# First channel tile of a layer's modulation: dot products moved from VectorE to TensorE

## The chip, the cores and the metric

The kernel runs on one core of a Trainium2 chip. Five engines work side by side: TensorE (PE in the profile, its weight loads PEld), VectorE (DVE), ScalarE (ACT), GpSimd (POOL) and SyncE (SP), which issues most of the transfers between the main memory and the on-chip memory. The metric is the device time of one execution in microseconds (us), lower is better; the median of three runs stands for a kernel.

## The reference

One layer of a latent generator over 512 tokens (8 rows by 64 columns) and 256 context tokens, 1024 channels, fp32 throughout. What matters here is how it opens:

```python
m = silu(c) @ w_mod + b_mod                 # (3072,) -> shift, scale, gate; the same with c_ctx
h  = rmsnorm(x,   pre_g) * (1 + sc)   + sh      # x: 512 x 1024
hc = rmsnorm(ctx, pre_g) * (1 + sc_c) + sh_c    # ctx: 256 x 1024
parts = split(h @ w_in)                     # 1024 x 10240: conv branch, q, k, v, gates
# gated short convolution; neighbourhood attention with rotary, bias and the context's keys;
# two output projections, sigmoid merge, @ w_o, rmsnorm, x + gate * ...
```

Scale and shift are one number per channel. In the kernel channels lie on the 128 partitions, eight channel tiles k = 0 to 7, so tile k needs 128 scales and 128 shifts, each a sum over 1024 products of silu(c) and a column of `w_mod`.

## The kernel before, in words

Weights and activations are split into two parts of a rounded fp32 format (H the rounded value, L the rest), and a projection is three products: H times h, L times h, H times the rest of h. The first stage makes h and, while it does, the first six of the projection's 128-channel units; these accumulate in six PSUM banks `acc[0]` to `acc[5]` over the eight channel tiles.

**The opening.** It runs in a block whose order on PE, DVE, ACT and SP is the order in which it is written. SP loads four tiles of x (128 tokens by 1024 channels, 512 KB each), then `sp` (small vectors: gains, biases), then for k = 0, 1, 2 two slabs of the transposed `w_mod` (128 channels by 1024, 512 KB each, tiles `wm`; slab 8 + k for the scale, k for the shift) and the first weights `fraw` (384 KB). ACT loads the row `crow` of c and applies SiLU. `spread` (line 507) multiplies it by a column of ones, so that it stands on all 128 partitions, and `kept` (L511) copies that to `cb`. Each x tile is normed: the sum of squares (`square`: DVE for tiles 0 and 1, ACT for 2 and 3), `root` on ACT, `norm` (reciprocal and a multiplication: DVE, but ACT, L503, for tile 3). PE turns channel tiles 0 and 1 of each x tile (L539), four x tiles into one PSUM bank per channel tile. Between these stand products whose result nobody reads (`keep_busy`, L516, the identity times 256 columns of `cb`).

**One channel tile.** `condition(k, 0, [0])` and `[1]` (L412) are a DVE instruction each: slab times `cb`, summed along the row, with the bias as starting value; L546 multiplies the scale by the gain. `cast_first` (ACT, L441) makes H of the first weights, `rest_first` (DVE, L445) makes L. ACT applies scale and shift to the turned tile twice (L555), once rounded to h and once exact to `m`; DVE takes the difference (L556). Then `steps(k)` on PE: six products of H and h (L457), six of L and h (L460), six of H and the rest (L463). Behind it PE turns channel tile k + 2 (L450). DVE works one tile ahead: in round k it does the tile's L, the scale of tile k + 1, the rest of h, and at the start of the next round that tile's shift.

**Later.** The context's modulation uses the same DVE instruction with c_ctx (`modulate_c`), for the eight tiles in the order 5, 6, 7, 4, 0, 1, 2, 3, and loads slabs for k below 5 once more. Outside the ordered block a planner that works with costs and due times places the instructions.

The lines that matter in the opening:

```python
for k in range(3): load_slab(k); load_first(k)
...
condition(0, 0, [0])
for t in range(4): keep_busy(1 if t < 2 else 2); # turn x tile t, channel tiles 0 and 1
keep_busy(3)
for k in range(KT):
    cast_first(k); condition(k, 0, [1])
```

## Time and profile before

| what | us |
|---|---|
| median of three runs | 703.24 (702.34 to 703.30) |
| the profiled execution, its own time | 702.93 |
| span of the profile (first to last instruction) | 701.1 |
| between the two, outside the span | 1.8 |

In the rows that follow, a row of the chain of waits gives a start, a length and who was busy; a row of the timeline gives start, length, engine, line, operation, the tiles written and read, and how many instructions; square brackets hold the idle time ahead of it and what ended it. A tile's name stands before its arrow where it is written. A product of two fp32 operands appears as two PE records, and so as two passes; a turned tile as one. The end of a PE record lies after the point at which the next one starts, since products are pipelined.

### The profile page before, as it was taken

Reading aid. Unit: us, or ns where it says so; the run is one execution under the profiler, and the core shown is the slowest. Engines: PE = TensorE matmul, PEld = TensorE weight load, DVE = VectorE, ACT = ScalarE, POOL = GpSimd, SP = SyncE. Lnnn points to the kernel's source line nnn. Section 1 sums busy time; section 2 is a strip of 40 time slices with the busy share of each in tenths; the row PEclk is TensorE's granted clock in tenths of the full one; section 3 lists DMA queues with packets and bytes.
Section 4 is the critical chain, followed back from the end, with each engine's and each line's share of the span. In section 5 each row is a group of like instructions: output and inputs, shape, how many; then the busy total and the mean of one; then the engine's idle time right before and its main releaser. Section 6 shows DMA issues by size and latency. Waiting matters only on the chain.

```text
span 701.1 us, 12064 instructions
## 1 busy us (share of the span) xinstructions
PE 691.2 (99%) x4340; PEld 622.7 (89%) x4340; DVE 609.6 (87%) x1184; ACT 448.2 (64%) x905; POOL 66.6 (9%) x110
## 2 busy tenths in 40 slices
PE   7999999999999999999999999999999999999996
PEld 5888888899989999898999989999898899988885
DVE  6999998799898899977999697999799787775996
ACT  7568542677688677675877757788593444442563
POOL 0000003121040310403103113000000000000000
PEclk9999999999999999999999999999999999999999
DMA  9995854347264463553635436334464445660013
GB/s 352 406 352 189 310 177 125 76 115 189 76 151 110 112 178 121 112 149 81 164 120 136 110 105 160 95 113 135 148 229 136 143 148 176 225 241 30 31 61 120
DMA packets 51727, 108.84 MB, mean 155 GB/s; under 512 B 6610, under 2 KB 6866, under 8 KB 51668
## 3 DMA queue, kind: packets, MB, share of 16 engines
q1 hardware_dynamic: 43202, 92.73, 38.6%
q0 software_dynamic: 8320, 15.21, 10.9%
q8 instruction: 34, 0.56, 0.4%
q14 instruction: 25, 0.20, 0.1%
q10 hardware_dynamic: 146, 0.14, 0.1%
HBM read 87.60 MB, written 5.25 MB: 132 GB/s over the span
## 4 chain that ended last, share of the span: by engine, by line
PE 89%; DVE 6%; ACT 2%; DMA 1%; issue 1%; SPq 0%; ACTq 0%; DVEq 0%
PE ps L299 29%; PE ps L174 8%; PE ps L175 8%; PE ps L176 8%; PE ps L187 6%; PE ps L1042 5%; PE ps L779 3%; PE ps L760 3%; PE ps L192 3%; PE ps L723 3%; PE ps L206 2%; PE ps L457 2%; DVE w L71 2%; PE ps L460 2%; PE ps L463 2%; PE ps L211 1%
## 5 line engine op out<-in xcount | busy, mean ns | idle before, releaser
L71 DVE TENSOR_TENSOR w<-ring,w 128x512 fp32r<-128x512 f32 (+1 forms) x215 | 165.8, 788 | 29.2 <-ACT w L68 27.6
L68 ACT CAST w<-ring 128x512 fp32r<-128x512 f32 (+1 forms) x215 | 144.7, 706 | 67.6 <-PE ps L176 22.3
L299 PE MATMUL ps<-S,w 128*128 128x256 f32 x1152 | 146.2, 283 | 0.2 <-ACT g L315 0.2
L299 PEld LDWEIGHTS ps<-S,w 128*128 128x128 f32 x1152 | 141.7, 192 | 0.4 <-ACT g L315 0.4
L299 PE MATMUL ps<-h,w 128*128 128x256 f32 x864 | 112.6, 284 | 0.2 <-DVE tc L316 0.2
L299 PEld LDWEIGHTS ps<-h,w 128*128 128x128 f32 x864 | 108.0, 191 | 2.4 <-DVE tc L316 0.5
L174 PE MATMUL ps<-h,w 128*128 128x512 f32 x144 | 56.4, 391 | 0.0
L175 PE MATMUL ps<-h,w 128*128 128x512 f32 x144 | 56.2, 390 | 0.0
L176 PE MATMUL ps<-h,w 128*128 128x512 f32 x144 | 55.9, 389 | 0.0
L631 POOL DMA_DIRECT2D tc<-tb x32 | 28.6, 1047 | 285.9 <-DVE tc L629 186.1
L753 ACT ACTIVATE pt<-pt,z 128x512 f32<-128x512 f32 x64 | 43.0, 724 | 7.3 <-DVE z L751 7.1
L68 ACT CAST TH<-ps 128x512 fp32r<-128x512 f32 x64 | 35.8, 586 | 12.1 <-PE ps L760 12.1
L71 DVE TENSOR_TENSOR TL<-ps,TH 128x512 fp32r<-128x512 f32 x64 | 42.5, 681 | 1.0 <-ACT TH L68 0.6
L739 DVE CUSTOM_DVE_ANT_1 ps<-ps,bt 128x512 f32<-128x512 f32 x56 | 38.7, 693 | 4.5 <-PE ps L723 4.3
L760 PE MATMUL ps<-ident,pt 128*128 128x128 f32 x256 | 33.3, 273 | 0.0
L187 PE MATMUL ps<-w,h 128*128 128x512 f32 x128 | 32.4, 394 | 0.0
L176 PEld LDWEIGHTS ps<-h,w 128*128 128x128 f32 x144 | 27.0, 188 | 5.7
L174 PEld LDWEIGHTS ps<-h,w 128*128 128x128 f32 x144 | 27.0, 188 | 5.5
L175 PEld LDWEIGHTS ps<-h,w 128*128 128x128 f32 x144 | 27.0, 188 | 5.5
L746 ACT ACTIVATE pt<-ps,m 128x512 f32<-128x512 f32 x32 | 22.1, 690 | 14.3 <-DVE m L739 13.6
L760 PEld LDWEIGHTS ps<-ident,pt 128*128 128x128 f32 x256 | 29.2, 140 | 2.2 <-ACT pt L753 0.4
L187 PEld LDWEIGHTS ps<-w,h 128*128 128x128 f32 x128 | 23.2, 188 | 4.4
(251 smaller groups left out, 1378.4 us busy)
## 6 DMA issues: line engine op xcount, KB each, us to landing
ring<-in_win SPq DMA_DIRECT2D x148, 256.0 KB, 3.2
wm<-in_wmod SPq DMA_DIRECT2D x26, 512.0 KB, 7.8
ring<-in_wout SPq DMA_DIRECT2D x32, 256.0 KB, 3.1
bt<-in_rel SPq DMA_DIRECT2D x16, 256.0 KB, 2.7
tc<-tb POOLq DMA_DIRECT2D x32, 128.0 KB, 3.6
wg<-in_wmod SPq DMA_DIRECT2D x16, 256.0 KB, 3.3
B<-in_wo SPq DMA_DIRECT2D x8, 512.0 KB, 5.9
fraw<-in_wfirst SPq DMA_DIRECT2D x8, 384.0 KB, 8.5
```

What stands on the lines that cost most here:

```text
L68: cast = nc.scalar.copy(H, src)
L71: nc.vector.tensor_sub(L, src, H.bitcast(F32))
L174: nc.tensor.matmul(ps, lhsT=H[k][:, cs], rhs=mH[k], start=k == 0, stop=False)
L175: nc.tensor.matmul(ps, lhsT=H[k][:, cs], rhs=mL[k], start=False, stop=False)
L176: nc.tensor.matmul(ps, lhsT=L[k][:, cs], rhs=mH[k], start=False, stop=k == KT - 1)
L187: nc.tensor.matmul(ps, lhsT=mH[k][:, ts], rhs=both[k].rearrange("p a c -> p (a c)"), start=k == 0, stop=False, skip_group_check=True,)
L299: nc.tensor.matmul(ps, lhsT=w[:, x, k], rhs=act[y][k], start=start and k + o == 0, stop=k == 3 and o == 2, skip_group_check=True,)
L631: nc.gpsimd.dma_start(x[i::2], u[1 - i::2], accum_op=ALU.add, max_dma_last_dim=2048)
L739: nc.vector.tensor_tensor_reduce(out=s3, in0=s3, in1=bt[:, e::4 - e][:, 0:2], scale=-1.0, scalar=3.0e38, op0=ALU.add, op1=ALU.min, accum_o ...
L753: nc.scalar.mul(x, x, z[:, i:i + 1])
L760: nc.tensor.transpose(tp[:, c], pt[:, c * P:(c + 1) * P], ident)
L1042: nc.tensor.matmul(out, lhsT=a(x, k, ts), rhs=w[y][k // 2][:, k % 2, cols], start=start and k + o == 0, stop=k == 3 and o == 2, skip_group ...
```

## The change

For channel tile 0 the scale and shift of x and of the context come from TensorE. `w_mod` for these 128 scales and 128 shifts lies untransposed in a new input `wmod0` (input channels on partitions, eight blocks of 128); `columns` holds c and c_ctx as columns (128 by 8 by 2). SiLU is applied to `columns` on ACT, behind that of `crow`. `condition0` multiplies, for each of the eight blocks and for scale and shift, a 128 by 128 block of `wmod0` (as weights) by two columns: 16 fp32 products, summed in `acc[1]` (scales) and `acc[2]` (shifts), column 0 for x, column 1 for the context. `finish0` reads the sums: bias and gain by one DVE instruction for the scale, the bias by another for the shift.

What goes with it: the slabs of k = 0 are loaded as four transfers of 256 KB instead of two of 512 KB; ACT issues a second transfer (8 KB) before its SiLU; norm of x tile 3 is on DVE; the H of the first weights of k = 0 is made on DVE; `spread` writes to `acc[3]` and `acc[4]`; `kept` stands later on ACT; nine `keep_busy` products become six; the context's tile 0 takes `colc`, so its two DVE reductions and the second load of its two slabs are gone.

```diff
+        columns = st.tile([P, KT, 2], F32, name="columns")
+        slab0 = []
+        def load_slab0():
+            for i in range(2):
+                t = st.tile([P, D], F32, name="wm", bufs=6).rearrange("p (b v c) -> p b v c", b=4, v=2)
+                slab0.append(t)
+                for n in range(2):
+                    nc.sync.dma_start(t[:, 2 * n:2 * n + 2], wmod0[:, 4 * i + 2 * n:4 * i + 2 * n + 2])
+        def condition0(blocks):
+            for b in blocks:
+                for v in range(2):
+                    nc.tensor.matmul(
+                        acc[1 + v][:, :2], lhsT=slab0[b // 4][:, b % 4, v], rhs=columns[:, b], start=b == 0, stop=b == KT - 1
+                    )
...
-            nc.scalar.copy(H, raws[k])
+            if k == 0:
+                nc.vector.tensor_copy(H, raws[k])
+            else:
+                nc.scalar.copy(H, raws[k])
...
             nc.scalar.dma_start(crow, cc[0:1].rearrange("o (a n) -> o a n", a=2))
+            nc.scalar.dma_start(columns, ccol)
...
-            for k in range(3):
+            load_slab0()
+            load_first(0)
+            for k in range(1, 3):
...
             nc.scalar.activation(crow, crow, AF.Silu)
+            nc.scalar.activation(columns, columns, AF.Silu)
...
-                if i < 3:
-                    nc.vector.tensor_scalar(out=xn[i], in0=xn[i], scalar1=top, scalar2=None, op0=ALU.mult)
-                else:
-                    nc.scalar.mul(xn[i], xn[i], top)
+                nc.vector.tensor_scalar(out=xn[i], in0=xn[i], scalar1=top, scalar2=None, op0=ALU.mult)
...
-                ps = tps()
+                ps = acc[3 + i]
...
-            condition(0, 0, [0])
...
-            for t in range(4):
-                keep_busy(1 if t < 2 else 2)
-            keep_busy(3)
+            keep_busy(1)
+            turn_tile(0)
+            keep_busy(1)
+            turn_tile(1)
+            condition0((0, 1))
+            keep_busy(1)
+            condition0((2, 3))
+            turn_tile(2)
+            condition0((4, 5))
+            keep_busy(1)
+            condition0((6, 7))
+            turn_tile(3)
+            keep_busy(2)
...
+            def finish0(v):
+                nc.vector.tensor_scalar(
+                    out=cols[0, v][:, 0:1], in0=acc[1][:, v:v + 1], scalar1=bsc1[:, 0:1], scalar2=sp[:, PG:PG + 1],
+                    op0=ALU.add, op1=ALU.mult,
+                )
+                nc.vector.tensor_add(cols[0, v][:, 1:2], acc[2][:, v:v + 1], sp[:, BM:BM + 1])
+            finish0(0)
             for k in range(KT):
                 cast_first(k)
-                condition(k, 0, [1])
+                if k:
+                    condition(k, 0, [1])
+                    nc.vector.tensor_mul(cols[k, 0][:, 0:1], cols[k, 0][:, 0:1], sp[:, PG + k:PG + k + 1])
+                else:
+                    finish0(1)
...
         def modulate_c(k):
-            if k < 5:
-                load_slab(k)
-            condition(k, 1)
-            nc.scalar.mul(cols[k, 1][:, 0:1], cols[k, 1][:, 0:1], sp[:, PG + k:PG + k + 1])
+            if k:
+                if k < 5:
+                    load_slab(k)
+                condition(k, 1)
+                nc.scalar.mul(cols[k, 1][:, 0:1], cols[k, 1][:, 0:1], sp[:, PG + k:PG + k + 1])
```

How it moves the instructions, at two places. First TensorE, from the first turned x tile to the first products of `steps(0)`. Before, with `x_129` to `x_135` the four x tiles (`h_82` is the h of channel tile 0):

```order
L539 MATMUL ps<-ident,x_129 128x128 x2
L516 MATMUL ps<-cb,ident 128x256
L539 MATMUL ps<-ident,x_131 128x128 x2
L516 MATMUL ps<-cb,ident 128x256 x2
L539 MATMUL ps<-ident,x_133 128x128 x2
L516 MATMUL ps<-cb,ident 128x256 x2
L539 MATMUL ps<-ident,x_135 128x128 x2
L516 MATMUL ps<-cb,ident 128x256 x3
L457 MATMUL ps<-h_82,fH 128x512 x6
```

and now, with `x_133`, `x_135` and `x_137` x tiles 1 to 3:

```order
L560 MATMUL ps<-ident,x_133 128x128 x2
L413 MATMUL ps<-columns,wm 128x2 x4
L538 MATMUL ps<-cb,ident 128x256
L413 MATMUL ps<-columns,wm 128x2 x4
L560 MATMUL ps<-ident,x_135 128x128 x2
L413 MATMUL ps<-columns,wm 128x2 x4
L538 MATMUL ps<-cb,ident 128x256
L413 MATMUL ps<-columns,wm 128x2 x4
L560 MATMUL ps<-ident,x_137 128x128 x2
L538 MATMUL ps<-cb,ident 128x256 x2
L478 MATMUL ps<-h_82,fH 128x512 x6
```

Between the turn of x tile 1 and that of x tile 3 stood four fillers; now 16 products of two columns and two fillers stand there.

Second VectorE, from the scaling of x tile 2 to the scale of channel tile 1 (ISA is the reduction, its second row reads the sum out). Before:

```order
L501 TENSOR_SCALAR x_133<-x_133,tops 128x1024
L499 RECIPROCAL tops<-tops 128x1
L412 ISA junk,col_188<-wm,cb,bsc_115 128x1024
L412 ISA col_188 128x1
L412 ISA junk,col_188<-wm,cb,sp 128x1024
L412 ISA col_188 128x1
L546 TENSOR_TENSOR col_188<-col_188,sp 128x1
L445 TENSOR_TENSOR fL<-fraw,fH 128x768
L412 ISA junk,col_217<-wm,cb,bsc_115 128x1024
```

and now:

```order
L525 TENSOR_SCALAR x_135<-x_135,tops 128x1024
L524 RECIPROCAL tops<-tops 128x1
L525 TENSOR_SCALAR x_137<-x_137,tops 128x1024
L579 TENSOR_SCALAR col_223<-ps,bsc_116,sp 128x1
L583 TENSOR_TENSOR col_223<-ps,sp 128x1
L460 CAST fH<-fraw 128x768
L579 TENSOR_SCALAR colc<-ps,bsc_116,sp 128x1
L583 TENSOR_TENSOR colc<-ps,sp 128x1
L466 TENSOR_TENSOR fL<-fraw,fH 128x768
L430 ISA junk,col_233<-wm,cb,bsc_116 128x1024
```

The two reductions of tile 0 are gone; the scaling of x tile 3, the four small reads of the sums and the cast of the first weights have come in, and the cast stands behind the first two reads, which need the last of the 16 products.

## The prediction

> **What bounds the kernel now.** I read the page first, then TensorE's busy time from the first `steps` product to the end of the projections, and last what TensorE waited for in that stretch (waited in total, times, longest).

> ```profile
> span 701.1 us, 12064 instructions
> PE 691.2 (99%) x4340; PEld 622.7 (89%) x4340; DVE 609.6 (87%) x1184; ACT 448.2 (64%) x905; POOL 66.6 (9%) x110
> ...
> 14.58:690.00 675.42, 675.05 (x4276) 1.00 0.50 152
> ...
> PE ps L299 <- DVE tc L316: 0.2, 1, 0.2
> PE ps L299 <- ACT g L315: 0.2, 1, 0.2
> ```

> From 14.58 us on TensorE is busy 675.05 of 675.42 us. What VectorE, ScalarE or the queues are spared behind that point is worth at most these 0.4 us. So the change is worth what it does to the start of `steps(0)`, and to the first rounds if they then stall. That start is read from the chain of waits over the opening:

> ```profile
> 0.74 0.52 ACTq L468
> ...
> 1.29 1.28 ACT L479
> ...
> 2.59 1.06 ACT crow L479
> ...
> 3.69 3.78 PE ps L507 x4
> 7.47 1.15 PE ps L516 x2
> 8.62 0.43 PE ps L539 x2
> 9.05 0.85 PE ps L516 x2
> 9.90 0.43 PE ps L539 x2
> 10.33 1.64 PE ps L516 x4
> 11.97 0.22 PE ps L539 x2
> 12.19 0.87 PE ps L516 x4
> 13.05 0.22 PE ps L539 x2
> 13.27 1.30 PE ps L516 x6
> ...
> 14.58 1.65 PE ps L457 x6
> ```

> The chain never leaves TensorE from 3.69 on. Two records of L516 (one filler) take 0.85 at 9.05, and four take 0.87 at 12.19: near 11.9 us the passes become twice as fast. The granted clock does not show it (1.00 throughout):

> ```profile
> 3.69:14.58 10.89, 10.88 (x31) 6.61 (x31) 8.58 (x18) 8.58 (x16) 0.00 (x0) 1.00 1.02 406
> ```

> The last three fillers hide something else: ScalarE's cast and h.

> ```profile
> 9.50 0.17 DVE L529 TENSOR_SCALAR bsc<-sp 128x8 f32<-128x8 f32 x1 [0.63 <-DMA sp<-in_small]
> ...
> 9.77 0.75 DVE L501 TENSOR_SCALAR x<-x,tops 128x1024 f32<-128x1024 f32 x1
> ...
> 10.97 1.27 DVE L412 CUSTOM_DVE_ANT_0 junk<-wm,cb,bsc 128x1024 f32<-128x1024 f32 x1
> 11.09 1.15 ACT L503 ACTIVATE x<-x,tops 128x1024 f32<-128x1024 f32 x1 [0.23 <-DVE tops L499]
> ...
> 12.97 0.83 ACT L441 CAST fH<-fraw 128x768 fp32r<-128x768 f32 x1 [0.73 <-DMA fraw<-in_wfirst]
> ...
> 13.49 0.15 DVE L546 TENSOR_TENSOR col<-col,sp 128x1 f32<-128x1 f32 x1
> 13.75 0.78 ACT L555 ACTIVATE h<-ps,col 128x512 fp32r<-128x512 f32 x1
> 13.83 0.96 DVE L445 TENSOR_TENSOR fL<-fraw,fH 128x768 fp32r<-128x768 f32 x1 [0.19 <-ACT fH L441]
> ...
> 15.91 0.69 DVE L556 TENSOR_TENSOR h<-m,h 128x512 fp32r<-128x512 f32 x1
> ...
> 17.97 0.78 ACT L555 ACTIVATE h<-ps,col 128x512 fp32r<-128x512 f32 x1 [0.63 <-DVE col L546]
> ...
> 19.21 1.65 PE L457 MATMUL ps<-h,fH 128*128 128x512 f32 x6
> ```

> The cast waits for the weights' landing (12.97), h follows at 13.75 and ends at 14.53, and `steps(0)` starts at 14.58. `steps(1)` starts at 19.21, 4.63 later; its h was done at 18.75, so VectorE has 0.46 us in hand there.

> **The change part by part.**

> *A second transfer on ScalarE's queue.* The first issue holds ScalarE for 0.52 before the table load of SiLU. A second of the same length moves the chain behind it by 0.5 (nothing at best, if it overlaps): `spread` starts at 4.2. With the same two fillers and two turned tiles behind it, TensorE ends x tile 1 at 10.83 instead of 10.33. x tile 1 is scaled by then (VectorE scales tile 2 at 9.77). The quarters of the slab are no hindrance: between the landings of `sp` (9.50) and of the first weights (12.97) come 1,024 KB of slab and 384 KB of weights in 3.47 us, so a quarter of 256 KB takes 0.63 and they land near 10.1, 10.8, 11.4 and 12.0. SiLU of 16 columns, a few tenths, lies under `spread`.

> *The 16 products.* Each is two passes (L507 shows four records for two products), each with a load of 128 by 128 weights: 32 loads, and two columns to stream behind each. No row shows such a product. What a load costs when nothing else holds it is seen where TensorE starts after a wait:

> ```profile
> 7.40 0.50 PEld L516 LDWEIGHTS ps<-cb,ident 128*128 128x128 f32 x2 [1.50 <-issue]
> ...
> 4.71 0.33 PEld L507 LDWEIGHTS ps<-crow,ones 1*128 1x128 f32 x1 [0.52 <-issue]
> ...
> 14.58 0.30 PEld L457 LDWEIGHTS ps<-h,fH 128*128 128x128 f32 x2 [0.41 <-ACT h L555]
> ...
> L457 PEld LDWEIGHTS ps<-h,fH 128*128 128x128 f32 x48 | 8.5, 189 | 1.9 <-ACT h L555 0.4
> ```

> Two loads end 0.30 after the first began, one alone lasts 0.19: the second began 0.11 after the first. Before 11.9 it is 0.50 less 0.33, or 0.17. Bounds for a pass: zero below, and above 0.30, a load of 0.19 plus 0.11 if nothing overlapped (the products would then end past 21, worse than the late clock below, with whose chance I count it). I take 0.17 until 11.9 and 0.11 after, since it is the load that no two columns can hide.

> From 10.83 to 11.9 that is 6 passes; the other 26 take 2.86; two fillers (0.87) and x tile 2 (0.22) stand among them. The last product ends at 11.9 + 2.86 + 0.87 + 0.22 = 15.85. Before, TensorE was done with x tile 3 at 13.27. The 26 fast passes alone are dearer than the two fillers they replace.

> [...]

> *From the sums to the steps.* `finish0(0)` is two small instructions (0.17 at 9.50, 0.15 at 13.49): 16.17. ScalarE's h (0.78) ends at 16.95, where `steps(0)` starts; x tile 3 and the two last fillers (0.22 + 0.87) end at 16.94 and cost nothing. That is 2.4 later than 14.58. Scaling x tile 3 on VectorE, 0.75 instead of 1.15, is of no use: the turn of tile 3 waits behind the products, not for it.

> *The cast behind the sums.* On VectorE the cast stands behind `finish0(0)`, and so do the other two reads, L, and everything for channel tile 1. For 768 elements I take 0.56 (three quarters of the 0.75 at 9.77; the dearest row is 0.96, the subtraction): done at 16.73, hidden by h. With the context's two reads (0.32) L starts at 17.05. Before, it was 4.92 from the start of L (13.83) to the end of h of tile 1 (18.75); the same now gives 21.97. TensorE would want it at 16.95 + 4.63 = 21.58. It stalls 0.4, and `steps(1)` starts at about 21.97 instead of 19.21: **2.75 later**. The rest of h for tile 0 (2.08 + 0.69 behind L's start) comes at 19.8, when the third group asks for it. After that the stall is over: VectorE's round is shorter than TensorE's 4.63, as the same reduction a round later shows (22.62 less 18.66, 3.96).

> ```profile
> 18.66 1.28 DVE L412 CUSTOM_DVE_ANT_0 junk<-wm,cb,bsc 128x1024 f32<-128x1024 f32 x1
> ...
> 22.62 1.28 DVE L412 CUSTOM_DVE_ANT_0 junk<-wm,cb,bsc 128x1024 f32<-128x1024 f32 x1
> ```

> *What is taken away.* Two reductions of 1.28 for x lay beside TensorE's fillers; two for the context and 1 MB of loads lie in the stretch where TensorE waits 0.4 in all. I count nothing, and 0.4 either way for the planner's new order there. On SP, the slabs of k = 3 now wait for TensorE's products (until 15.9) instead of VectorE's reductions to release the first two buffers, and hold the loads queued behind them; they are wanted three rounds of 4.63 after `steps(0)`. No cost; if that cover were gone, each us of lateness would be a us.

> The sum: 702.93 + 2.75 = 705.7 for the profiled execution, which lies 0.3 under the median; against the median 703.24, 706.0. Own range 705.0 to 707.2 (a pass of 0.10 to 0.13, cast up to 0.96, the queue's 0.5 away, 0.4 for the order).

> **The rivals.**

> *Late clock, or loads that nothing hides.* If two-column passes do not keep TensorE busy enough for the faster rate, all 32 passes cost 0.17 (5.4), the two fillers 1.7 and x tile 2 0.43: the products end at 18.4 and `steps(0)` starts at 19.5, 4.9 late; should the slow rate last into the steps, up to 4.3 us of them (7.47 to 11.9 is what it lasted under the fillers) run at half speed, 2.2 more. For it: the switch came only after that long stretch of full-width work. Against: over half of such a stretch is still there, from 7.97 to 10.83. 708 to 710.3.

> [...]

> *Cheap passes.* A load record of the turned tiles is 0.05 shorter than 0.19 in the fast part; a pass at 0.06 (and 0.12 before 11.9) would make 9 and 23 passes, the products end at 14.4, and VectorE's chain (0.32 + 0.56 + 0.32 + 4.92) gives `steps(1)` 20.5, 1.3 late: 704.5.

> *Not slower: the products vanish behind the landings.* If a pass costs nearly nothing and the faster rate comes early, the sums are done with the last quarter, near 12.5, and the landing of the first weights decides: cast 12.97 to 13.53, L at 13.85, h of tile 1 at 18.77 against TensorE's 13.6 + 4.63. `steps(1)` starts at 18.8, 0.4 early: 702.8. It decides as soon as the products end before 12.65. Against it: the loads would have to vanish, where the rows show 0.11 at the least; even then the two fillers and x tile 2 behind 10.83 (0.85, some 0.3, 0.43) leave them done at 12.4 only.

> **How the numbers follow.** My sum 0.55; late clock 0.15; cheap passes 0.18; vanished 0.12. The time is 706.0. The range runs to 703.3 and to 708.6: it leaves out most of the last rival and the worse half of the late clock. No change means within 0.2%, about 1.4 us, what a measurement of this kernel can tell: my sum and the late clock are slower, with a little of the cheap passes, 0.73; cheap and vanished mostly no change, 0.23; faster would need 1.4 us, more than any part above gives, 0.04.

> **What would show it.** The row of the products: 32 records, loads about 0.11 apart after the switch. `spread` at 4.2. The last product near 15.9, `steps(0)` near 17.0, an idle of some tenths before `steps(1)` put down to ScalarE's h, itself waiting for VectorE; behind that TensorE as full as before. I am wrong if the products' loads lie closer than 0.08, if `steps(0)` starts before 16.0, or if time appears behind 27 us.

## The result, and the profile after

| | before | after |
|---|---|---|
| median, us (runs beside each other) | 702.99 (702.34 to 703.30) | 712.80 (710.66 to 712.94) |
| the profiled execution, its own time | 702.93 | 712.94 |
| its span | 701.1 | 711.2 |
| start of `steps(0)` | 14.58 | 21.79 |
| start of `steps(1)` | 19.21 | 27.91 |
| from the start of `steps(1)` to the end of the span | 681.9 | 683.3 |

The change makes the kernel slower: ratio 1.0134, 95% interval [1.0113, 1.0155]. Of the 10.1 us by which the span grew, 8.7 lie ahead of `steps(1)`, and 1.4 behind it.

The opening first. These are TensorE's rows of the timeline after, from the first `spread` to `steps(1)`, and two rows of ScalarE and three of VectorE (start, length, engine, line, operation, tiles, count, and in brackets the idle time ahead and what ended it):

```profile
4.36 3.77 PE L529 MATMUL ps<-crow,ones 1*128 1x512 f32 x4 [4.36 <-ACT crow L503]
6.04 0.21 ACT L504 ACTIVATE columns<-columns 128x16 f32<-128x16 f32 x1 [1.73 <-DMA columns<-in_ccol]
8.57 1.19 PE L538 MATMUL ps<-cb,ident 128*128 128x256 f32 x2 [0.43 <-ACT cb L533]
...
11.26 1.71 PE L413 MATMUL ps<-columns,wm 128*128 128x2 f32 x8
12.83 1.20 PE L538 MATMUL ps<-cb,ident 128*128 128x256 f32 x2
13.82 1.71 PE L413 MATMUL ps<-columns,wm 128*128 128x2 f32 x8
15.39 0.67 PE L560 MATMUL ps<-ident,x 128*128 128x128 f32 x2
15.85 1.71 PE L413 MATMUL ps<-columns,wm 128*128 128x2 f32 x8
17.41 1.20 PE L538 MATMUL ps<-cb,ident 128*128 128x256 f32 x2
18.41 1.71 PE L413 MATMUL ps<-columns,wm 128*128 128x2 f32 x8
...
19.98 0.67 PE L560 MATMUL ps<-ident,x 128*128 128x128 f32 x2
20.23 0.55 DVE L460 CAST fH<-fraw 128x768 fp32r<-128x768 f32 x1
20.43 1.91 PE L538 MATMUL ps<-cb,ident 128*128 128x256 f32 x4
20.47 0.78 ACT L603 ACTIVATE h<-ps,col 128x512 fp32r<-128x512 f32 x1 [8.64 <-PE ps L560]
20.95 0.95 DVE L466 TENSOR_TENSOR fL<-fraw,fH 128x768 fp32r<-128x768 f32 x1
21.79 3.12 PE L478 MATMUL ps<-h,fH 128*128 128x512 f32 x6
24.71 1.62 PE L481 MATMUL ps<-h,fL 128*128 128x512 f32 x6
...
27.91 1.64 PE L478 MATMUL ps<-h,fH 128*128 128x512 f32 x6
```

TensorE waits for nothing from 8.57 on; it is simply slow. Within a group the passes of the products start 0.213 apart (only the first is followed after 0.07), in all four groups alike: seven such steps and 0.07 are the 1.57 from 11.26 to 12.83. The fillers among them (L538) are at half rate too, and so is the first group of `steps(0)`: 3.12 for six records, where before it took 1.65 (14.58). Only in the second group, near 24.8, does the rate double. Before, that had happened near 11.9.

Now the part behind the opening, in the table by stretch (length, busy time of TensorE with its count, then the other engines), before and after:

```profile
28.00:680.00 652.00, 651.63 (x4172) 592.12 (x4171) 572.09 (x1109) 421.71 (x858) 65.91 (x104) 1.00 0.49 148
```

```profile
28.00:680.00 652.00, 650.55 (x4168) 590.53 (x4167) 566.73 (x1104) 419.18 (x850) 65.92 (x104) 1.00 0.49 147
```

and what TensorE waited for there after (total, times, longest):

```profile
PE ps L176 <- DVE w L71: 1.4, 2, 1.1
```

TensorE is idle 1.45 us now and was idle 0.37 before. That is 1.1 of the 1.4 behind `steps(1)`.

### The profile page after: what moved, and what is told of

It reads as the page before. It is cut to its first block, busy times and chain, and to the rows that moved or that the text cites. A ratio compares the mean times of both kernels' runs of the same rounds, so it can differ in the third digit from the quotient of the medians.

```text
span 711.2 us, 12103 instructions
## 1 busy us (share of the span) xinstructions
PE 699.2 (98%) x4366; PEld 630.0 (89%) x4366; DVE 606.6 (85%) x1181; ACT 446.7 (63%) x904; POOL 66.6 (9%) x110
## 4 chain that ended last, share of the span: by engine, by line
PE 91%; DVE 3%; DMA 2%; ACT 2%; issue 1%; SPq 0%; ACTq 0%; DVEq 0%
PE ps L299 34%; PE ps L176 7%; PE ps L174 7%; PE ps L175 7%; PE ps L187 6%; PE ps L1091 5%; PE ps L828 4%; PE ps L809 4%; PE ps L192 3%; PE ps L772 3%; PE ps L206 2%; PE ps L478 2%; PE ps L481 2%; DMA ring<-in_win 1%; PE ps L484 1%
## 5 line engine op out<-in xcount | busy, mean ns | idle before, releaser
L71 DVE TENSOR_TENSOR w<-ring,w 128x512 fp32r<-128x512 f32 (+1 forms) x215 | 166.1, 791 | 28.4 <-ACT w L68 27.6
L299 PE MATMUL ps<-S,w 128*128 128x256 f32 x1152 | 146.1, 283 | 0.0
L299 PEld LDWEIGHTS ps<-S,w 128*128 128x128 f32 x1152 | 141.7, 192 | 0.0
L299 PE MATMUL ps<-h,w 128*128 128x256 f32 x864 | 112.5, 284 | 0.0
L299 PEld LDWEIGHTS ps<-h,w 128*128 128x128 f32 x864 | 108.0, 191 | 2.0
L71 DVE TENSOR_TENSOR TL<-ps,TH 128x512 fp32r<-128x512 f32 x64 | 42.7, 684 | 0.9 <-ACT TH L68 0.5
```

What stands on the lines that cost most here:

```text
L71: nc.vector.tensor_sub(L, src, H.bitcast(F32))
L299: nc.tensor.matmul(ps, lhsT=w[:, x, k], rhs=act[y][k], start=start and k + o == 0, stop=k == 3 and o == 2, skip_group_check=True,)
```

## The experiments

The question of the first runs: why does the rate not turn? One theory says that two-column passes, each behind a load of 128 by 128 weights (after the change a load's record is 0.33 long, and loads and passes alike start 0.21 apart), are not work by which the rate is raised. Its rival says that the opening is late and has holes: the second transfer on ScalarE's queue lands late, the first filler starts at 8.57 instead of 7.4, and the rate follows from there.

**Wide passes.** The products stream 128 columns instead of 2. The 126 added ones are ones; the sums that are read are the same.

```diff
-        columns = st.tile([P, KT, 2], F32, name="columns")
+        columns = hp.tile([P, KT, P], F32, name="columns", tag="s1")
-                        acc[1 + v][:, :2], lhsT=..., rhs=columns[:, b], ...
+                        acc[1 + v][:, :P], lhsT=..., rhs=columns[:, b], ...
+            nc.vector.memset(columns[:, :, 2:], 1.0)
-            nc.scalar.dma_start(columns, ccol)
+            nc.scalar.dma_start(columns[:, :, :2], ccol)
-            nc.scalar.activation(columns, columns, AF.Silu)
+            nc.scalar.activation(columns[:, :, :2], columns[:, :, :2], AF.Silu)
```

> The changed kernel, but each of the 32 passes streams 128 columns instead of 2 (the other 126 are ones, and the sums of the first two are unaffected). In the slow part the weight load of a pass, 0.21 us, is as long as 128 columns, so a pass costs the same there. Theory A (passes that are nearly all weight load do not count as work for TensorE's faster rate): the rate now changes about 4 to 5 us after the first filler, near 12 to 13.5 us, passes are then 0.11 apart, steps(0) starts near 16.5 to 18 instead of 21.7, and the kernel is 4 to 6 us faster than the changed one (707 to 709). Theory B (the late change of rate is chance or comes from the idle time before the first filler): no gain, 712 to 713, rate change still near 24.

Measured: 710.94 us, ratio 1.0107 [1.0092, 1.0122]. The edit had a cost of its own: the transfer writes 2 of every 128 columns of the wide tile (8 bytes in a piece, by the tile's shape), and ScalarE waited 7.2 us for it, where it waited 1.73 after the change. The first filler starts at 14.04 instead of 8.57. What followed it is the answer (timeline, TensorE):

```profile
14.04 1.19 PE L539 MATMUL ps<-cb,ident 128*128 128x256 f32 x2 [5.87 <-ACT cb L534]
...
16.74 1.61 PE L413 MATMUL ps<-columns,wm 128*128 128x128 f32 x8
...
18.61 1.05 PE L413 MATMUL ps<-columns,wm 128*128 128x128 f32 x8
...
23.23 1.66 PE L478 MATMUL ps<-h,fH 128*128 128x512 f32 x6
```

Near the end of the first group of products the rate doubles, 3.9 us after the first filler, and `steps(0)` runs at the full rate from its start. It begins 1.4 us later than after the change and yet `steps(1)` begins at the same time, 27.90.

**Narrow fillers in the kernel before.** The other way round: nothing of the change, but the fillers stream 2 columns instead of 256, and there are twice as many.

```diff
-                for _ in range(n):
-                    nc.tensor.matmul(acc[5][:, :256], lhsT=ident, rhs=cb[:, 0, :256], start=True, stop=True)
+                for _ in range(2 * n):
+                    nc.tensor.matmul(acc[5][:, :2], lhsT=ident, rhs=cb[:, 0, :2], start=True, stop=True)
```

> The kernel before, but each filler of 256 columns becomes two fillers of 2 columns: the same time in the slow part (two products of two passes at 0.21), nearly all of it weight load, and no other work in the opening. Theory A: the rate no longer changes at 11.9 but some 4 us into the steps; turning x tile 3 ends later than 13.3, steps(0) starts 0.5 to 2 late and its first 3 to 4 us run at half rate; 2 to 4 us slower than before (705 to 707). Theory B: the rate changes near 12 as before, the time stays within 0.5 us of before (703).

Measured: 706.33, ratio 1.0042 [1.0027, 1.0057]. TensorE's timeline:

```profile
7.42 1.01 PE L516 MATMUL ps<-cb,ident 128*128 128x2 f32 x4
...
13.98 2.56 PE L516 MATMUL ps<-cb,ident 128*128 128x2 f32 x12
16.40 2.91 PE L457 MATMUL ps<-h,fH 128*128 128x512 f32 x6
19.10 2.76 PE L460 MATMUL ps<-h,fL 128*128 128x512 f32 x6
21.66 1.97 PE L463 MATMUL ps<-h,fH 128*128 128x512 f32 x6
...
23.82 1.64 PE L457 MATMUL ps<-h,fH 128*128 128x512 f32 x6
```

The kernel before, with its opening as early as ever, shows the fault of the changed one: 9 us of narrow passes (7.42 to 16.40), with only the turned tiles between them, left the rate at half, and the first two groups of the steps took 2.91 and 2.76 where 1.65 and 1.56 stood before. A late start was not needed for that.

**The second transfer out of the way.** `columns` loaded by SP ahead of x, so that ScalarE's queue has one transfer as before.

```diff
-            nc.scalar.dma_start(columns, ccol)
+            nc.sync.dma_start(columns, ccol)
```

> The changed kernel, but the 8 KB of columns are loaded by SP ahead of the x tiles instead of by ScalarE. The wait of 1.7 us on ScalarE ahead of SiLU of the columns should go, and with it the late copy of cb and the idle 0.4 us before the first filler; x tiles land 0.4 to 0.5 later. Theory A: the first filler starts 0.4 to 0.7 earlier and all behind it too, about 712.2. Theory B (the idle time before the first filler costs the early change of rate): rate change near 13, 705 to 708.

Measured: 712.60, ratio 1.0126 [1.011, 1.0143]. The first filler starts at 7.41, as early as before; the products start at 10.94 (0.24 of waiting for a quarter of the slab) and take as long, `steps(0)` starts at 21.63, `steps(1)` at 27.43. The hole ahead of the first filler is worth 0.5 us of the 8.7.

**Wide passes without the late transfer.** As the wide passes, but c and c_ctx are loaded into a small tile of their own, as in the changed kernel, and SiLU writes them into the wide one. Against the wide passes:

```diff
+        narrow = st.tile([P, KT, 2], F32, name="narrow")
-            nc.scalar.dma_start(columns[:, :, :2], ccol)
+            nc.scalar.dma_start(narrow, ccol)
-            nc.scalar.activation(columns[:, :, :2], columns[:, :, :2], AF.Silu)
+            nc.scalar.activation(columns[:, :, :2], narrow, AF.Silu)
```

> The changed kernel with 128 columns per pass again (126 of them ones), and the two real columns loaded compactly, as in the changed kernel, then spread by SiLU, so that the first filler is not held up. Theory A (a pass that is nearly all weight load does not count for the faster rate): first filler near 8.6, rate change 4 us later near 12 to 13.5, products done near 16 to 17, steps(0) at 17 to 18 at full rate, steps(1) near 22 instead of 27.9; 706 to 708. Theory B (chance, or the idle time): steps(1) stays near 27.9.

Measured: 705.15, ratio 1.0030 [1.0019, 1.0042], a little under what was expected. TensorE's timeline:

```profile
8.43 1.19 PE L540 MATMUL ps<-cb,ident 128*128 128x256 f32 x2 [0.57 <-ACT cb L535]
...
11.12 1.56 PE L414 MATMUL ps<-columns,wm 128*128 128x128 f32 x8
12.53 0.60 PE L540 MATMUL ps<-cb,ident 128*128 128x256 f32 x2
12.96 1.05 PE L414 MATMUL ps<-columns,wm 128*128 128x128 f32 x8
...
17.58 1.66 PE L479 MATMUL ps<-h,fH 128*128 128x512 f32 x6
...
22.25 1.66 PE L479 MATMUL ps<-h,fH 128*128 128x512 f32 x6
```

64 times as many columns, and 5.7 us earlier at `steps(1)`. The passes get 0.111 apart from 12.2 on (0.89 for the eight from 12.96 to 13.85). In this run the rate turns about when the prediction's sum has it turn: `steps(1)` at 22.25 where it had 21.97.

**The same kernel with 2 and with 32 columns a pass.** Both differ from the last one by a number only, so the staging of `columns` is the same in all; the diff shows 32, the other has 2 in the same two places.

```diff
-                        acc[1 + v][:, :P], lhsT=..., rhs=columns[:, b], ...
+                        acc[1 + v][:, :32], lhsT=..., rhs=columns[:, b, :32], ...
```

> e5 with 2 columns per pass: the staging, the tile's place and everything else of e5 kept, so that it differs from e5 in the width of the passes alone (and in what the planner makes of it). Theory A: the opening of the changed kernel again, rate change near 24, steps(1) near 27.9; 709 to 713 by the tail. If e5's gain came from the staging or the tile's place, it stays near e5's 705.2. The tail behind steps(1) was 681 to 682 us in the runs without a stall of TensorE near 105 us and 683.3 to 683.9 in those with it; lateness of the opening alone would bring the stall here again.

> e5 with 32 columns per pass instead of 128: a quarter of a pass streams. Theory A with a share that counts: if a quarter is enough, as e5 (rate change near 12.4, steps(1) near 22.2); if not, as the changed kernel (rate change near 24, steps(1) near 27.9).

Measured: 2 columns 711.72, ratio 1.0121 [1.0104, 1.0138]; 32 columns 712.13, ratio 1.0130 [1.0114, 1.0147]. In the timeline of 32 columns TensorE stays at half rate until 24.8, as in that of 2:

```profile
18.29 1.75 PE L414 MATMUL ps<-columns,wm 128*128 128x32 f32 x8
...
21.67 3.12 PE L479 MATMUL ps<-h,fH 128*128 128x512 f32 x6
24.59 1.64 PE L482 MATMUL ps<-h,fL 128*128 128x512 f32 x6
```

With that the width of the passes alone carries the opening: 22.25 for `steps(1)` with 128 columns, 27.82 with 32, 27.97 with 2.

**64 columns.** The same edit once more.

```diff
-                        acc[1 + v][:, :32], lhsT=..., rhs=columns[:, b, :32], ...
+                        acc[1 + v][:, :64], lhsT=..., rhs=columns[:, b, :64], ...
```

> As the kernel with 128 columns per pass and the copied columns, but the products stream 64 columns (the first 2 are the real ones, 62 are ones; the sums read are the same). 2 and 32 columns left the passes at 0.21 us and the slow rate to about 24.7, with steps(1) at 27.8 to 28.0; 128 columns turned the rate at about 12.4, with steps(1) at 22.25. Theory A (the passes count by the share of the time in which rows stream; at the slow rate 64 columns fill about half of a pass of 0.21): if half is enough, the passes get 0.11 to 0.13 apart from about 12.4 to 14 on, steps(1) starts at 22 to 23, and the span is 703 to 704. Theory B (only passes that fill their time count): as with 32 columns, passes of 0.21 throughout, steps(0) near 21.7, steps(1) near 27.8, span 710 to 711. Something between (the rate turning within the first group of steps) would speak for an average over a window. For the part behind steps(1): a span 681 us behind it if the planner's order leaves TensorE no wait near 105 us, 682.7 to 684 if it does.

Measured: 705.18, ratio 1.0037 [1.0023, 1.0051], and the executions fall into two groups, seven from 704.9 to 706.1 and two at 709.2. The profiled one is of the second group:

```profile
18.47 1.81 PE L414 MATMUL ps<-columns,wm 128*128 128x64 f32 x8
20.07 0.64 PE L562 MATMUL ps<-ident,x 128*128 128x128 f32 x2
20.49 1.55 PE L540 MATMUL ps<-cb,ident 128*128 128x256 f32 x4
21.70 1.74 PE L479 MATMUL ps<-h,fH 128*128 128x512 f32 x6
```

Here the products stay at 0.213, but the rate doubles within the last two fillers, near 21.5, 3.2 us earlier than with 32 columns. The first group has no profile; its times are those of 128 columns. So 64 columns seem to be on the border, enough in some executions and not in others. By an estimate from the rows, a pass of 64 columns leaves TensorE without rows to stream for about half of its 0.213, since passes of 128 columns at half rate are as far apart (two turned tiles take 0.43, from 10.89 to 11.32).

**Fillers between the products taken out.** Is it that the fillers stand in the wrong place?

```diff
             condition0((0, 1))
-            keep_busy(1)
             condition0((2, 3))
             turn_tile(2)
             condition0((4, 5))
-            keep_busy(1)
             condition0((6, 7))
```

> The changed kernel without the two fillers between the products. Theory A: the fillers there bring no faster rate and cost 0.85 each: the products end 1.7 earlier, steps(0) starts near 20.0, the rate changes some 3 us behind it as before, steps(1) near 26.2; 711 to 711.5. If the fillers hold the rate up in part, the rate changes later and the gain is under 1 us.

Measured: 711.63, ratio 1.0116 [1.0075, 1.0156]. `steps(0)` starts at 20.02 and `steps(1)` at 26.20: in the profiled execution 1.7 us are gained up to there, the time of two fillers at half rate, and the first group of the steps is as slow (3.12). The four executions scatter from 707.9 to 714.2, so the time alone says little. The two fillers cost 1.7 and bring the rate nothing.

**Early fillers, in the kernel after and in the one before.** `keep_busy` multiplies the identity by itself, so that it can run from 1.36 on; four of them stand ahead of `spread`. In the kernel after the two among the products go.

```diff
-                    nc.tensor.matmul(acc[5][:, :256], lhsT=ident, rhs=cb[:, 0, :256], start=True, stop=True)
+                    for _ in range(2):
+                        nc.tensor.matmul(acc[5][:, :P], lhsT=ident, rhs=ident, start=True, stop=True)
+            keep_busy(4)
             wide = [spread(i) for i in range(2)]
```

> The changed kernel, with four double fillers of the identity on itself (no data to wait for) ahead of spread, all fillers on the identity, and no fillers between the products. Theory A: full-width work starts near 1.5 us, the rate changes once a few us of it are counted; if spread's one-row passes count, that is by 6 to 9 us, the products (0.11 a pass) end by 13 to 14 and steps(0) starts by 14.5 to 15.2, steps(1) by 19.2 to 20; 702.5 to 705 with the planner's order as the unknown. If spread's passes do not count either, the rate changes only 4 us behind the fillers at 8 and the products end near 15.5, steps(1) at 21; 705 to 706.5. Theory B: no earlier than the changed kernel, 711 to 713.

> The kernel before with the same early fillers on the identity. Its steps(0) waits for the cast behind the first weights' landing (12.97), not for TensorE: steps(0) stays at 14.5 and the time at 703.4 within 0.7, whatever the rate does. If the rate were what holds it, it would gain 0.4 or more.

Measured: in the kernel after 709.22, ratio 1.0085 [1.007, 1.01]; in the kernel before 703.50, ratio 1.0002 [0.9993, 1.0011]. Both expectations missed in the opening. In the kernel after, the products stay at half rate and `steps(1)` starts at 26.91, not by 21; of the 3.3 us that its span is shorter, only 1.0 lie ahead of `steps(1)`. In the kernel before, `spread` now waits behind the early fillers (5.07 instead of 3.69), and `steps(0)` starts at 16.36, not at 14.5. The median is unchanged all the same; the executions fall into two groups, three from 701.9 to 702.2 and seven from 703.4 to 704.1, and the profiled one is of the second. The timeline of the second kernel:

```profile
1.36 3.78 PE L517 MATMUL ps<-ident 128*128 128x128 f32 x16 [1.36 <-POOL ident masks.py:199]
5.07 3.78 PE L507 MATMUL ps<-crow,ones 1*128 1x512 f32 x4
8.78 1.22 PE L517 MATMUL ps<-ident 128*128 128x128 f32 x4
...
13.63 1.41 PE L517 MATMUL ps<-ident 128*128 128x128 f32 x8
```

3.7 us of full-width fillers and 3.7 us of `spread` behind them, with no hole, do not turn the rate; it turns at 14.4, 5.6 us after the start of the fillers that follow `spread`. The passes of `spread` stream 512 columns but use one row of the 128. It looks as if they count for as little as the narrow ones, but no run changed that alone.

**Eight early fillers, wide passes, and the rest put right.** The attempt at a version that beats both: the wide passes with their own staging, eight of the early fillers ahead of `spread` instead of four, none among the products, the copies of `kept` last on ScalarE's part of the norms, the cast ahead of `finish0`. The core of it:

```diff
+            keep_busy(8)
             wide = [spread(i) for i in range(2)]
...
-            kept(0, wide[0])
...
             norm(3)
+            kept(0, wide[0])
             kept(1, wide[1])
...
+            cast_first(0)
             finish0(0)
```

> The changed kernel with 128 columns per pass (staged as in e5), full-width fillers of the identity on itself from the start without a break (eight double ones) and spread behind them, no fillers between the products, the copies of spread behind the roots on ScalarE, and the cast of the first weights ahead of the reads of the sums on VectorE. Theory A: an unbroken stretch of full-width work from 1.4 us brings the faster rate by 5 to 8.5 us, so spread takes 0.9 instead of 3.8, the products start with the first quarter (10.2 to 11) at 0.11 a pass and end near 14, steps(0) starts near 15.2 and steps(1) near 19.9 against 19.21 before; with a tail (steps(1) to the end) of 681 to 684 us the time is 702.5 to 705.5. If the rate is still slow at 8.5, spread takes 3.4 to 3.8 and steps(1) is at 22 or later: 705 to 708.

Measured: 704.84, ratio 1.0013 [1.0001, 1.0025], in two groups again: four executions from 702.7 to 703.1, six from 704.8 to 705.5. The profiled one is of the first group:

```profile
1.36 5.57 PE L541 MATMUL ps<-ident 128*128 128x128 f32 x32 [1.36 <-POOL ident masks.py:199]
6.86 1.98 PE L531 MATMUL ps<-crow,ones 1*128 1x512 f32 x4
...
10.20 1.95 PE L414 MATMUL ps<-columns,wm 128*128 128x128 f32 x16
...
15.28 1.66 PE L479 MATMUL ps<-h,fH 128*128 128x512 f32 x6
...
19.93 1.64 PE L479 MATMUL ps<-h,fH 128*128 128x512 f32 x6
```

The rate doubles at 5.0, within the early fillers, and holds. Even so, with the sums at the full rate from start to end, `steps(1)` starts at 19.93, 0.7 later than before the change, and by the median no time is gained; the faster group lies within the times of the kernel before (702.4 to 704.4). In this form the products on TensorE are worth no more than the reductions on VectorE that they replace.

**The context's tile 0 back on VectorE.** For the 1.4 us behind `steps(1)`: `finish0(1)` goes, and the two reductions and the loads of the context's tile 0 come back.

```diff
-                    finish0(1)
+                    pass
...
-            if k:
-                if k < 5:
-                    load_slab(k)
-                condition(k, 1)
+            if k < 5:
+                load_slab(k)
+            condition(k, 1)
```

> The changed kernel, but the context's tile 0 gets its scale and shift from VectorE again, with the second load of its two slabs; the products still sum both columns, of which the context's is not read. The stalls of TensorE near 71, 75 and 106 us (about 1.8 us in all, 1.3 of it at 106) either go, if they come from the order into which the missing context work let the planner move the rest: 711 to 711.5; or stay or grow, if they come from VectorE and the loads being late since the opening: 712.8 to 714. The opening is unchanged: steps(0) at 21.7.

Measured: 713.78, ratio 1.0148 [1.0133, 1.0163]. TensorE waits for VectorE's `w` (L71) 1.2 us as it did after the change (1.4), so the part taken from the context is not the cause. What was expected puts a time like this down to the lateness of the opening; the runs together say otherwise. From the start of `steps(1)` to the end of the span, in us (the last column has one letter for each order of VectorE's instructions in the traces; a dash is an order that no other run has):

| run | `steps(1)` at | the rest | TensorE's wait for L71 there | VectorE's order |
|---|---|---|---|---|
| after | 27.9 | 683.3 | 1.4 | A |
| context back on VectorE | 27.9 | 683.7 | 1.2 | - |
| `columns` by SP | 27.4 | 683.5 | 1.6 | A |
| no fillers among the products | 26.2 | 683.9 | 1.8 | A |
| 2 columns, own staging | 28.0 | 682.8 | 0.9 | A |
| 32 columns | 27.8 | 682.7 | 0.8 | - |
| wide passes, late transfer | 27.9 | 681.0 | none | B |
| 64 columns | 26.4 | 681.0 | none | - |
| early fillers, after | 26.9 | 681.0 | none | B, but for one instruction |
| wide passes | 22.3 | 681.0 | none | B |
| eight early fillers, wide passes | 19.9 | 681.1 | none | - |
| before | 19.2 | 681.9 | none | C |
| narrow fillers, before | 23.8 | 681.8 | 0.2, at L779 | C |
| early fillers, before | 21.0 | 681.2 | none | - |

The wait does not follow the lateness of the opening: with `steps(1)` at 27.9 it is there after the change and not there in the wide passes, and among the four runs of order A it is longest (1.8) where `steps(1)` is earliest (26.2). It comes and goes with the order in which the planner places the rest: all four runs of order A wait, none of the three of order B does, and their rest is 681.0 whether `steps(1)` starts at 22.3 or at 27.9. That order changes with many edits of the opening, even between passes of 2 and of 128 columns. What it looks like after the change, in VectorE's timeline and in TensorE's:

```profile
99.28 0.43 DVE L71 TENSOR_TENSOR hc<-ctT,hc 128x256 fp32r<-128x256 f32 x1 [1.82 <-ACT hc L68]
...
102.14 1.28 DVE L430 CUSTOM_DVE_ANT_0 junk<-wm,cb,bsc 128x1024 f32<-128x1024 f32 x1
...
103.68 1.28 DVE L430 CUSTOM_DVE_ANT_0 junk<-wm,cb,sp 128x1024 f32<-128x1024 f32 x1
...
104.89 2.36 DVE L71 TENSOR_TENSOR w<-ring,w 128x1024 fp32r<-128x1024 f32 x2
...
106.16 0.50 PE L176 MATMUL ps<-h,w 128*128 128x512 f32 x1 [1.09 <-DVE w L71]
```

and in the wide passes with the late transfer:

```profile
98.47 1.28 DVE L430 CUSTOM_DVE_ANT_0 junk<-wm,cb,sp 128x1024 f32<-128x1024 f32 x1
...
99.67 1.22 DVE L71 TENSOR_TENSOR w<-ring,w 128x1024 fp32r<-128x1024 f32 x1
```

After the change the splitting of the projection's weights (L71) stands behind context reductions that go on to 104.9, with 1.82 us of VectorE's waiting for ScalarE ahead of them; in the other kernel they end at 99.7. Which of the planner's decisions does that stays open: no run fixed the order there. Nor is it shown why the rest of the kernel before is 0.9 longer than 681.0; its idle time (0.37) is less than half of that.

## Why the prediction was wrong

The direction was right (slower, 0.73), the size was not: 706.0 with 703.3 to 708.6, against 712.8. What happened is the rival called the late clock, which had 0.15 and 708 to 710.3, and on top of it 1.4 us behind the opening; the rival too was priced too low, with `steps(0)` at 19.5 where 21.79 was measured. In the order of the prediction's steps:

- **The step that failed** is the choice "0.17 until 11.9 and 0.11 after", which takes over from the kernel before the moment of the switch. Before, the fillers and turned tiles in a row, from 7.40 on, brought that moment about (narrow fillers there put it off to 22.5); the change breaks this row off with two-column passes. With them the switch came at 24.8, and the runs with 2, 32 and 128 columns show that the width decides. The prediction's argument against the late clock, that over half of the full-width stretch remains (7.97 to 10.83), does not hold: in the kernel after, the full-width stretch from 8.57 to 11.26 was broken off by narrow passes and did not turn the rate.
- **The price of a pass at half rate** was too low: 0.213 apart, not 0.17. The prediction's own chain had it: two turned tiles, each with its own load, 0.43 at 8.62 and at 9.90. With the seams at each group's end 32 passes took 6.27 from start to start (four times 1.57: 11.26 to 12.83 and so on) where the sum had 3.88: 2.4 more. The two fillers among them took 2.0 instead of 0.87, and x tile 2 0.46 instead of 0.22: 1.4 more. What follows x tile 1 started at 11.26; the prediction had 10.83: 0.4 (10.83 is an end by the chain, some 0.2 behind such a start; start against start it is 0.6, of which 0.2 were in hand at h). Together 4.2. The passes of 2 columns, each with its own load of 128 columns, stand 0.213 apart at half rate. At the full rate no run has narrow passes; those of 128 columns stand 0.111 apart there, where the prediction had 0.11.
- **What covers h.** The prediction let h end last (16.95) and the last fillers fit under it. At half rate x tile 3 and the fillers take 1.81 (19.98 to 21.79) instead of 1.09 and end after h (20.47 + 0.78 = 21.25). 0.7 more. The sum so far is 16.95 + 4.2 + 0.7 = 21.8, as measured.
- **The steps at half rate.** From `steps(0)` to `steps(1)` 6.12 instead of the 5.02 predicted with VectorE's stall; the stall itself did not come, since TensorE was late enough. 1.1 more. The prediction had "2.2 more" for this in the rival. 4.2 + 0.7 + 1.1 is 6.0, the distance between 21.97 and 27.91 to 0.1.
- **Behind the opening** "0.4 either way for the planner's new order" was too narrow: 1.4. Over the runs this part lies between 681.0 and 683.9, and in the shortest it is 0.9 less than before, more than the 0.4 that the prediction held possible.
- **The second transfer**: `spread` at 4.36, where 4.2 was forecast. But that SiLU of `columns`, counted as lying under `spread`, waits 1.73 for its data was not seen: the 8 KB land 4.7 us after their issue. It delays everything on ScalarE behind it and leaves TensorE idle for 0.43.
- **Right** were the cast on VectorE (0.55; 0.56 forecast), the chain from L's start to the end of h of tile 1 (20.95 to 25.86, 4.91; 4.92 forecast), the 32 records, and, in the one run where the rate turns about as it assumes, the opening as a whole: with wide passes `steps(0)` and `steps(1)` start 0.6 and 0.3 from the forecast. That it comes so close is in part luck, since `steps(0)` is 0.6 late and the forecast stall of 0.4 ahead of `steps(1)` does not come; and the time, 705.15, has a rest that is 0.9 shorter than before.

How much full-width work it took, the traces show run by run. From the start of an unbroken stretch of passes of 128 columns or more (`spread` not counted) to the doubling took 3.7 us (eight early fillers), 3.8 and 3.9 (the two wide runs), 4.1 (`columns` by SP), 4.4 (before), 4.7 and 4.8 (context back on VectorE, 2 columns), 4.9 (after, 32 columns, no fillers), 5.6 and 5.9 (early fillers, before and after) and 6.2 (narrow fillers). The profiled run of 64 columns is the exception: the rate doubles 1.5 us after its last product, which suggests that some of those passes counted. No one length fits them all: a stretch of 3.7 us was not enough with four early fillers, and with eight it was. Why the one was enough and the other not was not shown, nor why the executions of one kernel fall into two groups, as with 64 columns: only one execution of each kernel was profiled.

## What to carry to other kernels

Where TensorE's opening runs at half rate, ask of every pass that stands there how wide it streams: here a pass of 2 columns behind a load of 128 took as long as one of 128 columns (0.213), and passes of 2 and of 32 columns left the rate at half until 24.8, where those of 128 had it doubled at 12.2. If such products can't be avoided, widen them with columns that nobody reads: here that alone took 1.0121 to 1.0030. And when a term of a prediction is a moment ("the rate turns at 11.9"), ask what brings that moment about, and whether the change removes it.
